# Storing a bias table's rows 128 times to read them on a diagonal, in place of products with a flipped identity

## The chip, the cores and the metric

The kernel runs on one core of a Trainium2 chip. The core has a matrix engine (TensorE, PE in the profile), a vector engine (VectorE, DVE), an activation engine (ScalarE, ACT), a general engine (GpSimd, POOL) and a sync engine (SyncE, SP), which here does little but issue transfers. Each engine works through its own list of instructions in order; semaphores hold an instruction until what it needs is there. Transfers between the memory of the chip (DRAM) and the on-chip memory (SBUF, 128 partitions) are carried by 16 DMA engines.

The metric is the device time of one execution, in microseconds, the median over several runs.

## The reference, cut to what matters

One layer of an encoder over 512 tokens of width 2048, float32. Two branches run side by side: a gated linear recurrence in eight heads, and an attention that lets each query see the 128 keys that an indexer picks for it. The change touches one term of the attention only, the bias by relative position:

```python
bias_table = rel_bias.astype(F32)                      # 32 buckets x 8 heads
...
logits = jnp.einsum('bthd,btkhd->bthk', q_blk, k_sel).astype(F32) * B_HEAD_DIM ** -0.5
bias = jnp.moveaxis(bias_table[t5_bucket(top_idx - t_pos[None, :, None])], -1, 2)
logits = jnp.where(valid[:, :, None, :], logits + bias, -jnp.inf)
```

For a head, the bias of query t and key s depends on s - t alone, and beyond a certain distance it is constant. So a row of 384 values per head holds all that is not constant, and a block of 128 queries by 256 keys needs that row shifted by one place from query to query: B[p, c] = row[127 - p + c].

## The kernel before, in words

All matrix products are made in pieces that keep float32 precision: each operand is split into a high and a low half, and three products (high x high, high x low, low x high) are summed in PSUM. The lines 74 to 76 are these three products, line 79 a single one. The halves of a weight piece are made by ACT (line 70, the high half) and DVE (line 71, the low half) from a raw tile (`wr`, two of them) that SP loads in line 127. The split halves have three places. A raw tile's next load is issued when DVE has made the low half of the piece that was in it; a piece is split while PE works on the piece two before it.

The program is one list of jobs, each a large product. Between the pieces of a job a function `pump` is called, which issues loads, flushes stores that were put off (`late`), and takes one step of each of several lanes: the recurrence's heads (`hgrn`), the top-k of the indexer (`top`), the attention (`att`), norms, and `t5`, the bias table. The lanes' instructions so fall between the products in the engines' lists, in the order in which Python emits them; nothing reorders them later.

The bias table is made while PE works on the jobs `ai_job(3)`, `ai_job(2)`, `af_aq(0)` and `af_aq(1)`, whose pieces are 48 products of 256 columns or 24 of 512 columns. At the same time the head pairs 3 and 2 of the recurrence run (tiles `hl`, `hz`, `hq`, `hqk`), and DVE runs the rounds of top-k (MAX and MATCH_REPLACE on tile `M`). The lane `t5` does this: it makes the eight rows by a product with one-hot buckets (lines 436 to 440, tile `tl`, 8 partitions x 384), splits them, stores both halves in DRAM, reads them back with the query's index as the partition (line 450; a pitch of one element between the partitions, so that partition p starts at element p), and multiplies by a flipped identity (line 457), since the wanted shift falls with p instead of rising. The result, a block of 128 x 256 for each of eight heads, goes to DRAM (`bh_d`, line 460). There are four rounds of two heads each, a pair of products in each.

Later the attention of each head loads its block (line 964), and POOL adds it to the mask (lines 968 and 971).

## Time and profile before

| | |
|---|---|
| median of 3 runs | 1338.1 us (1338.05 to 1338.66) |
| the profiled execution, its own time | 1337.35 us |
| its span in the profile | 1335.5 us |
| TensorE busy | 1324.8 us, 99% |
| VectorE busy | 1066.9 us, 80% |
| ScalarE busy | 669.2 us, 50% |
| GpSimd busy | 35.6 us, 3% |
| share of the chain that ended last on PE | 96% |
| bytes moved by the transfers | 205.82 MB |

The profile is of one execution. Its page gives the busy time of each engine, the transfers by queue, and the chain of work that ended last, followed back from the last instruction: an engine's share of that chain says how far it sets the time. The rows of a view in order of time give start and duration in us, engine, line, operation, the tiles written and read, and in brackets how long the engine stood idle before and what ended that. "SPq" rows are the issues of transfers, not the transfers themselves. Buffer numbers are left out of names, so that `t_d` is the tensor `t5_d`, `t` the lane's PSUM bank, and `hl`, `hz` banks of the recurrence.

### The profile page before, as it was taken

How to read it: one execution, taken by the hardware profiler on the slowest of the kernel's cores; microseconds unless marked ns; L12 is line 12 of the kernel's file. 1: busy time of each engine (PE TensorE's matmuls, PEld its weight loads, DVE VectorE, ACT ScalarE, POOL GpSimd, SP SyncE). 2: the span in 40 equal slices, each digit the busy share in tenths (PEclk: the TensorE clock that was granted, in tenths of full speed). 3: DMA queues.
4: the chain of work that ended last, by engine and by line, in shares of the span. 5: the costliest groups of instructions: out<-in, count | busy, mean ns of one | idle time of the engine just before them, and what ended most of it. 6: DMA issues, size and time to landing. Idle time of an engine off the chain costs nothing.

```text
span 1335.5 us, 26569 instructions
## 1 busy us (share of the span) xinstructions
PE 1324.8 (99%) x10876; PEld 1233.8 (92%) x10876; DVE 1066.9 (80%) x1705; ACT 669.2 (50%) x1064; POOL 35.6 (3%) x54
## 2 busy tenths in 40 slices
PE   9999999999999999999999999999999999999997
PEld 8988999999999999999999888888888888899996
DVE  7777888998888888886778988875656758899856
ACT  6455555554454444444666465656434423444435
POOL 2000000000000000000000000021001000000000
PEclk9999999999999999999999999999999999999999
DMA  6344545443454444434523624445655556643564
GB/s 241 92 113 115 158 142 159 144 142 111 143 158 143 142 143 142 130 111 163 184 86 102 182 76 155 132 144 182 239 192 191 186 175 219 204 160 126 164 209 163
DMA packets 141290, 205.82 MB, mean 154 GB/s; under 512 B 8672, under 2 KB 82032, under 8 KB 141040
## 3 DMA queue, kind: packets, MB, share of 16 engines
q1 hardware_dynamic: 140592, 203.78, 48.2%
q8 instruction: 85, 1.39, 0.4%
q10 hardware_dynamic: 576, 0.35, 0.1%
q14 instruction: 37, 0.30, 0.1%
HBM read 168.42 MB, written 35.68 MB: 153 GB/s over the span
## 4 chain that ended last, share of the span: by engine, by line
PE 96%; DVE 2%; DMA 1%; ACT 1%; issue 0%; SPq 0%; DVEq 0%; ACTq 0%
PE pp L76 15%; PE pp L74 15%; PE pp L75 15%; PE acc L74 14%; PE acc L76 14%; PE acc L75 14%; PE hl L79 1%; PE ho L79 1%; DMA xt<-in_x_t_dram 1%; PE sc L75 1%; PE sc L74 1%; PE sc L76 1%; DVE xl L338 0%; PE hp L79 0%; PE po L76 0%; PE po L75 0%
## 5 line engine op out<-in xcount | busy, mean ns | idle before, releaser
L149 ACT ACTIVATE bh<-wr 128x768 fp32r<-128x768 f32 x128 | 108.2, 846 | 208.5 <-issue 99.8
L151 ACT ACTIVATE wh<-sv 128x512 fp32r<-128x512 f32 x256 | 152.6, 624 | 86.1 <-DVE sv L144 65.5
L74 PE MATMUL pp<-sh,wh 128*128 128x256 f32 x618 | 170.6, 276 | 0.0
L75 PE MATMUL pp<-sl,wh 128*128 128x256 f32 x618 | 170.6, 276 | 0.0
L76 PE MATMUL pp<-sh,wl 128*128 128x256 f32 x618 | 170.6, 276 | 0.0
L71 DVE TENSOR_TENSOR wl<-wr,wh 128x1024 fp32r<-128x1024 f32 (+1 forms) x104 | 125.4, 1207 | 56.3 <-ACT wh L70 56.3
L153 DVE TENSOR_TENSOR wl<-sv,wh 128x1024 fp32r<-128x1024 f32 x128 | 156.4, 1222 | 6.3 <-ACT wh L151 0.3
L152 DVE TENSOR_TENSOR bl<-wr,bh 128x768 fp32r<-128x768 f32 x128 | 122.2, 954 | 43.4 <-ACT bh L149 43.2
L70 ACT ACTIVATE wh<-wr 128x1024 fp32r<-128x1024 f32 (+1 forms) x104 | 108.2, 1040 | 92.2 <-PE acc L75 44.1
L74 PE MATMUL acc<-xh,wh 128*128 128x512 f32 x304 | 120.3, 396 | 0.0
L76 PE MATMUL acc<-xh,wl 128*128 128x512 f32 x304 | 118.5, 390 | 0.0
L75 PE MATMUL acc<-xl,wh 128*128 128x512 f32 x304 | 118.5, 390 | 0.0
L75 PEld LDWEIGHTS pp<-sl,wh 128*128 128x128 f32 x618 | 116.0, 188 | 0.0
L76 PEld LDWEIGHTS pp<-sh,wl 128*128 128x128 f32 x618 | 116.0, 188 | 0.0
L74 PEld LDWEIGHTS pp<-sh,wh 128*128 128x128 f32 x618 | 116.0, 188 | 0.0
L74 PE MATMUL pp<-xh,bh 128*128 128x256 f32 x416 | 114.8, 276 | 0.0
L76 PE MATMUL pp<-xh,bl 128*128 128x256 f32 x416 | 114.8, 276 | 0.0
L75 PE MATMUL pp<-xl,bh 128*128 128x256 f32 x416 | 114.8, 276 | 0.0
L74 PE MATMUL acc<-yh,wh 128*128 128x512 f32 x256 | 100.3, 392 | 0.0
L75 PE MATMUL acc<-yl,wh 128*128 128x512 f32 x256 | 99.7, 390 | 0.0
L76 PE MATMUL acc<-yh,wl 128*128 128x512 f32 x256 | 99.7, 389 | 0.0
L144 DVE TENSOR_TENSOR sv<-wr 128x512 f32<-128x512 f32 x128 | 87.8, 686 | 9.0 <-DMA wr<-in_w_in_dram 6.5
(404 smaller groups left out, 3612.2 us busy)
## 6 DMA issues: line engine op xcount, KB each, us to landing
wr<-in_w_in_dram SPq DMA_DIRECT2D x136, 512.0 KB, 3.7
wr<-in_w_out_dram SPq DMA_DIRECT2D x32, 512.0 KB, 3.8
mg<-gate_d SPq DMA_DIRECT2D x48, 256.0 KB, 4.1
gate_d<-c SPq DMA_DIRECT2D x44, 256.0 KB, 4.9
wr<-in_w_in_dram SPq DMA_DIRECT2D x36, 256.0 KB, 3.0
wr<-in_w_pa_dram SPq DMA_DIRECT2D x16, 512.0 KB, 4.8
wr<-in_w_pb_dram SPq DMA_DIRECT2D x16, 512.0 KB, 3.9
wr<-in_w_qidx_dram SPq DMA_DIRECT2D x8, 512.0 KB, 3.7
```

The source lines that it names most:

```text
L70: A.activation(hi, src, AF.Copy)
L71: V.tensor_tensor(lo, src, hi.bitcast(F32), op=OP.subtract)
L74: PE.matmul(ps, lh, rh, start=first, stop=False, skip_group_check=True)
L75: PE.matmul(ps, lh, rl, start=False, stop=False, skip_group_check=True)
L76: PE.matmul(ps, ll, rh, start=False, stop=last, skip_group_check=True)
L79: PE.matmul(ps, l, r, start=first, stop=last, skip_group_check=True)
L144: V.tensor_tensor(sv[:, 0:2, :], b[:, 1:3, :], b[:, 0:1, :].to_broadcast([128, 2, 256]), op=OP.add)
L149: A.activation(bh, b[:, 1:4, :], AF.Copy)
L151: A.activation(vh[:, i:i + 2, :], sv[:, i:i + 2, :], AF.Copy)
L152: V.tensor_tensor(bl, b[:, 1:4, :], bh.bitcast(F32), op=OP.subtract)
L153: V.tensor_tensor(vl, sv, vh.bitcast(F32), op=OP.subtract)
```

## The change

The lane `t5` ends earlier. The rows `tl` are not split; one transfer stores each of them 128 times, into a DRAM tensor of 1024 rows of 384 elements. A head then reads its block from there with a pitch of 383 elements from partition to partition, starting at element 127 of its first copy: element p * 383 + 127 + c is element 127 - p + c of copy p. The flipped identity, its load and the eight products with it, the eight reads in the lane, four copies out of PSUM and four stores go.

```diff
-    t5_d = dram.tile([2, H, 384], F32, name="t5_d")
+    t5_d = dram.tile([H * 128, 384], F32, name="t5_d")
...
-    bh_d = dram.tile([H, 128, 256], F32, name="bh_d")
...
-        raw = R.i.tile([128, 512], F32, name="nt", bufs=2)
-        SP.dma_start(raw[:, 0:384], c_buckets)
-        SP.dma_start(raw[:, 384:], c_flip)
...
-        A.activation(flip, raw[:, 384:], AF.Copy)
...
         V.tensor_scalar(tl, ps[:H, :384], far, None, op0=OP.subtract)
         yield
-        split(*ts, tl)
-        for i in range(2):
-            late[1].append(lambda i=i: SP.dma_start(t5_d[i], ts[i].bitcast(F32)))
-        for _ in range(3):
-            yield
-        for h in range(0, H, 2):
-            bf = R.i.tile([128, 2, 2, 256], FR, name="bf")
-            for i in range(2):
-                SP.dma_start(bf[:, i].bitcast(F32), bass.AP(tensor=t5_d.tensor, offset=t5_d.offset + (i * H + h) * 384,
-                                                            ap=[[1, 128], [384, 2], [1, 256]]))
-            yield
-            yield
-            yield
-            ps = bank("t5")
-            for i in range(2):
-                mm(ps, flip, bf[:, i].rearrange("p h c -> p (h c)"), i == 0, i == 1)
-            e = R.i.tile([128, 2, 256], F32, name="nt", bufs=2)
-            V.tensor_copy(e, ps.rearrange("p (h c) -> p h c", h=2))
-            late[1].append(lambda h=h, e=e: SP.dma_start(bh_d[h:h + 2].rearrange("h p c -> p h c"), e))
-            yield
+        late[1].append(lambda: SP.dma_start(t5_d.rearrange("(h p) c -> h p c", h=H), tl.unsqueeze(1).to_broadcast([H, 128, 384])))
+        yield
...
         bh = R.a.tile([128, 256], F32, name="bh")
-        SP.dma_start(bh, bh_d[h])
+        SP.dma_start(bh, bass.AP(tensor=t5_d.tensor, offset=t5_d.offset + h * 128 * 384 + 127, ap=[[383, 128], [1, 256]]))
```

SP's list at the place of the table, before (`wr` are weight loads, `hg` a load of gates for the recurrence):

```order
L426 DMA rb<-in_rel_bias_dram 32x8
L428 DMA nt<-in_buckets_dram 128x384
L429 DMA nt<-in_flip_dram 128x128
L127 DMA wr<-in_w_in_dram 128x4x256 x3
L444 DMA t_d<-tlh 8x384
L444 DMA t_d<-tll 8x384
L450 DMA bf<-t_d 128x2x256 x2
L127 DMA wr<-in_w_in_dram 128x4x256 x2
L450 DMA bf<-t_d 128x2x256 x2
L127 DMA wr<-in_w_in_dram 128x4x256
L460 DMA bh_d<-nt 128x2x256
L127 DMA wr<-in_w_in_dram 128x4x256
```

and now, where the lines above the change have moved up by one and those below by 23:

```order
L423 DMA rb<-in_rel_bias_dram 32x8
L425 DMA raw<-in_buckets_dram 128x384
L126 DMA wr<-in_w_in_dram 128x4x256 x3
L437 DMA t_d<-tl 1024x1x384
L126 DMA wr<-in_w_in_dram 128x4x256 x5
L718 DMA hg<-gate_d 128x2x512
```

The wide store stands where the two small ones stood, behind the third of these weight loads, and the next five weight loads follow it with nothing between.

ACT's list a little later, now, is as it was but for the line numbers (`hz` to `hqk` and the two after it are steps of a recurrence head, `hv` is the result of the last piece of `ai_job(2)`):

```order
L70 ACTIVATE hzh<-hqk 128x512 x2
L70 ACTIVATE wh<-wr 128x1024
L871 ACT_TABLE_LOAD
L876 ACTIVATE hqk<-hz,cols 128x512 x2
L877 ACTIVATE hqk<-hqk 128x1024
L70 ACTIVATE wh<-wr 128x1024
```

Here nothing moved: the high half of a weight piece stands ahead of the head's steps, before as now.

## The prediction

> **What bounds the kernel now.** I read the head of the page first, then the chain of waits, then the stretch in which the bias table is made.

> ```profile
> span 1335.5 us, 26569 instructions
> ...
> PE 1324.8 (99%) x10876; PEld 1233.8 (92%) x10876; DVE 1066.9 (80%) x1705; ACT 669.2 (50%) x1064; POOL 35.6 (3%) x54
> ...
> q1 hardware_dynamic: 140592, 203.78, 48.2%
> ...
> PE 96%; DVE 2%; DMA 1%; ACT 1%; issue 0%; SPq 0%; DVEq 0%; ACTq 0%
> ```

> TensorE sets the end: it is busy for 99% of the span and 96% of the chain that ended last is its own work. An edit gains only what it takes out of PE's stream, and loses whatever makes PE stand still. The stretches around the bias table (columns: time, then the busy us of PE, of the weight loads, of DVE, ACT and POOL) show the second thing to watch:

> ```profile
> 690.00:863.00 173.00, 173.00 (x2236) 151.77 (x2235) 149.63 (x289) 99.76 (x151) 2.85 (x5) 1.00 0.42 126
> 722.00:753.00 31.00, 31.00 (x270) 28.97 (x270) 29.96 (x73) 15.53 (x22) 0.00 (x0) 1.00 0.48 135
> ```

> PE never stands still there, but between 722 and 753 us DVE is busy for 29.96 of 31.00 us. Whatever holds DVE up in that stretch can't be caught up before PE next needs it.

> **What the change removes.** On PE eight products with the flipped identity, in four pairs. Instructions by form for their bank, then PE in order of time around the second pair:

> ```profile
> L79 PE MATMUL t<-bf,flip x8: 392/392/503, 728.7 to 768.4; 128*128 128x512 f32 x8
> L459 DVE COPY nt<-t x4: 679/681/714, 730.9 to 770.0; 128x512 f32<-128x512 f32 x4
> ```

> ```profile
> 741.08 0.62 PE L79 MATMUL t<-bf,flip 128*128 128x512 f32 x2
> 741.54 0.28 PE L74 MATMUL acc<-wh,xh 128*128 128x256 f32 x1
> ```

> The 392 ns of one product is its way through the array and overlaps the next; what the pair costs is the distance to the following start, 741.54 - 741.08 = 0.46 us. Four pairs: **1.85 us off PE**. (The other three stand behind short products, after which the next start is late with or without them; I take 0.46 for each.) On DVE four copies of 0.68 us go, on ACT and DVE the flip's copy and one split, on SP fifteen transfers: eight reads and four stores of 256 KB, two stores of 12 KB, the flip's load:

> ```profile
> bf<-t_d SPq DMA_DIRECT2D x8, 256.0 KB, 4.3
> ...
> bh_d<-nt SPq DMA_DIRECT2D x4, 256.0 KB, 4.3
> ...
> t_d<-tlh SPq DMA_DIRECT2D x1, 12.0 KB
> ```

> Beside these products, which go themselves, PE waits for none of that in this stretch, so it is worth nothing by itself; the copy at 744.69 us will matter below, since it shortens DVE's queue by 0.68 us.

> **What it adds.** One transfer: 8 rows of 1536 bytes, each written 128 times, 1024 pieces and 1.57 MB, issued from eight partitions where nearly all others move 128. SP's queue in order of time (start, duration, line; x2 joins two issues, here at 722.10 and 728.20), and a weight load's time to landing:

> ```profile
> 713.34 0.37 SPq L127 DMA_DIRECT2D wr<-in_w_in_dram  x1
> 713.75 0.44 SPq L444 DMA_DIRECT2D t_d<-tlh  x1
> 714.25 0.29 SPq L444 DMA_DIRECT2D t_d<-tll  x1
> ```

> ```profile
> 717.49 0.90 SPq L450 DMA_DIRECT2D bf<-t_d  x2
> 722.10 6.48 SPq L127 DMA_DIRECT2D wr<-in_w_in_dram  x2
> 735.80 0.37 SPq L127 DMA_DIRECT2D wr<-in_w_in_dram  x1
> ```

> ```profile
> wr<-in_w_in_dram SPq DMA_DIRECT2D x136, 512.0 KB, 3.7
> ```

> The new store takes the place of the two small ones, at 713.75 us. The load of 713.34 is ahead of it and lands near 713.34 + 3.7 = 717.0, so the store's bytes flow from about 716.5 us. The next weight load (722.10, call it A) and the one after it (728.20, B) stand behind it in the same queue.

> How long does it take? The page's queue row gives 0.482 x 16 x 1335.5 us / 140592 = 73 ns for a mean packet of 1449 bytes, that is 19.8 GB/s for one engine's stream, and 79 us for the store if it came out as one stream, 40 as two, 20 as four, 9.9 as eight. **Bounds:** not under 9.9 us, since eight source rows make at most eight streams of that kind; not much over 79 us, since in the ordinary 128-row transfers each of 16 streams serves eight rows, so that one stream is what this trace has seen come out of eight rows. Nothing wide of the trace comes from so few rows; the two 12 KB stores are too small to tell. Between ends eight-fold apart I take the middle, between two and four streams: **28 us**, from 716.5 to 744.6 us.

> [...]

> **Who waits for A.** ACT turns A into its high half, DVE into its low half, PE multiplies with both. ACT, PE and DVE in order of time:

> ```profile
> 723.29 1.05 ACT L70 ACTIVATE wh<-wr 128x1024 fp32r<-128x1024 f32 x1
> ...
> 732.17 1.06 ACT L70 ACTIVATE wh<-wr 128x1024 fp32r<-128x1024 f32 x1 [1.06 <-PE acc L76]
> 733.25 1.28 ACT L894 ACT_TABLE_LOAD   x1
> ```

> ```profile
> 744.36 0.39 PE L74 MATMUL acc<-xh,wh 128*128 128x512 f32 x1
> ```

> ```profile
> 752.61 0.73 PE L79 MATMUL hl<-hq,hqk 128*32 128x32 f32 x62
> ```

> ```profile
> 734.56 1.22 DVE L71 TENSOR_TENSOR wl<-wr,wh 128x1024 fp32r<-128x1024 f32 x1
> ...
> 744.69 0.68 DVE L459 COPY nt<-t 128x512 f32<-128x512 f32 x1
> ...
> 748.75 1.22 DVE L748 TENSOR_TENSOR hqk<-hq,hf 128x1024 f32<-128x1024 f32 x1
> ```

> Two raw weight tiles exist, so the ACT split at 723.29 is of the other tile and the one at 732.17 is of A. It waits there for the end of a piece of PE's (three split tiles exist), hence its result is for the piece after the next two, which PE starts at 744.36. A's 512 packets are 32 on each engine, 32 x 73 ns = 2.3 us. With the store's end at 744.6 A is in at 746.9 instead of at 722.10 + 3.7 = 725.8. ACT is in order: it stands from 732.2 to 746.9, with the table load and the four ACT steps of the head in progress queued behind. DVE stands at its own half of A from 734.6 on, with the top-k rounds, the scaling of the heads and L748 behind it. Then:

> - ACT's half is done at 746.9 + 1.06 = 748.0, DVE's at 748.0 + 1.22 = 749.2, where before it was 735.8: DVE is 13.4 us late.
> - PE, by then 0.9 us early by two pairs, wants A at 743.4 and waits about 5 us; it runs one piece and half of the next (about 8.5 us of products) and comes to the products of L79 that stood at 752.61. They need DVE's L748, which ended at 749.97; now 749.97 + 13.4 - 0.68 (the copy that is gone) = 762.7.
> - PE resumes 762.7 - 752.6 = 10.1 us later than before. Two pairs of the four still come: 0.9 us back. **Net loss 9.2 us.**

> After that PE sets the pace again: DVE waits for L79's products before its next scaling, and its lateness is PE's. What PE lost is not regained, since it has no idle time to give up.

> In general, for a store of L us the net is L - 18.9, as long as that is above -1.85: A lands within what ACT and DVE have to spare up to L = 17, and a loss over 0.2% of the time needs L over 21.6.

> **The bias reads.** The heads read 128 rows of 1 KB at a pitch of 1532 bytes instead of 1024: same count, same bytes.

> ```profile
> L964 SPq DMA_DIRECT2D bh<-bh_d x8: 418/450/528, 864.9 to 1042.6; - x8
> ...
> DMA to landing us min/median/max: 3.2/4.3/6.8
> ```

> ```profile
> POOL MB L968 <- DMA bh<-bh_d: 146.0, 6, 33.1
> ```

> Only POOL waits for them, which works for 3% of the span and whose sums are asked for two steps of the pump later. Should every read take double the 4.3 us, POOL still starts within the 33 us that it idles now. Worth nothing; without that cover it would be 4.3 us for each of eight heads. The first read, at 864.9 us, is 120 us behind the store's end.

> **Sum.** The profiled execution took 1337.35 us, 0.75 below the median of 1338.1. 1337.35 + 9.2 = 1346.6; against the median, **1347.3 us**. Its own range, with L from 22 to 33 us, is 1341 to 1352.

> **Rivals.**

> *The store hides* (not slower). Each source row is served as a stream of its own, L = 9.9, the store ends at 726.4, A is in by 729 and ACT finds it at 732.2. What is left is the 1.85 us off PE: 1336.2 us. For it: the other stores reach such speeds, and nothing shows a limit at the source rows. Against: no transfer in the trace has drawn on so few rows. It decides up to L = 17. [...]

> *A store in between*, L from 17 to 21.6: the loss eats the gain, 1336.2 to 1340.8 us.

> *One stream*, L = 79: the store ends near 796, A is 50 us later than in the forecast, and each us is PE's: about 1398 us. Little speaks for it, since eight rows going out through one stream would need the transfer to be dealt out by rows as the wide ones are.

> *Faster than the products alone explain*: 5 us of DVE, ACT and SP work goes from the densest stretch of DVE, and with a hidden store PE might find a step ready sooner. But PE stood still nowhere between 690 and 863 us, so there is nothing to find; it would need 0.8 us more, to 1335.4.

> **How the numbers follow.** About 0.2%, 2.7 us, is what a measurement of this kernel tells from no change. On the scale of streams, the doublings from 9.9 to 79 us put about six tenths above 21.6 and four below; I give the forecast 0.59, the single stream 0.04, the store in between 0.05, the hidden store 0.28 and the faster variant 0.04. Slower is 0.59 + 0.04 = 0.63, same 0.05 + 0.28 = 0.33, faster 0.04. The range takes in the hidden store at the one end and the forecast's own range at the other: 1335.7 to 1352; what is left out is the single stream, the faster variant and the forecast's edge.

> **What would show it.** In the changed kernel's profile: the store's time to landing, 28 us or so for right, near 12 for the hidden store. ACT's split near 732 us with some 15 us of idle time before it, put down to the weight load. PE with two gaps, about 5 us near 743 and a similar one at the products of L79 some 10 us later. If ACT finds A on time and PE has no gap, the length of the store was wrong. If the store is long and PE still has no gap, then the order of transfers in the queue was: A would have passed the store.

## The result, and the profile after

| | kernel before | changed kernel |
|---|---|---|
| median | 1338.07 us (1337.17 to 1338.66, 4 runs) | 1350.37 us (1349.81 to 1350.51, 4 runs) |
| profiled execution, its own time | 1337.35 us | 1350.3 us |
| span | 1335.5 us | 1348.5 us |

The ratio is 1.0092, with a 95% interval of 1.0074 to 1.0109: the change costs 12.3 us. The forecast was a loss of 9.2 us, to 1347.3 us, with a range of 1335.7 to 1352.

The head of the page of the changed kernel, and the engines' shares of the chain that ended last:

```profile
span 1348.5 us, 26522 instructions
...
PE 1327.6 (98%) x10868; PEld 1235.0 (92%) x10868; DVE 1063.5 (79%) x1700; ACT 668.1 (50%) x1062; POOL 38.1 (3%) x54
...
PE 92%; DVE 3%; DMA 3%; ACT 1%; issue 0%; SPq 0%; DVEq 0%; ACTq 0%
```

PE has eight products fewer and yet is busy longer, its share of the chain fell from 96 to 92%, and DMA has 3% of it instead of 1. The stretches by engine, in the same columns as before (time, busy us of PE, weight loads, DVE, ACT, POOL, then the granted clock, the share of DMA and GB/s):

```profile
690.00:863.00 173.00, 161.90 (x2166) 141.39 (x2165) 137.97 (x274) 86.45 (x133) 2.85 (x5) 0.97 0.40 106
722.00:753.00 31.00, 23.76 (x190) 22.36 (x189) 13.40 (x39) 7.75 (x13) 0.00 (x0) 0.90 0.48 74
```

PE stands for 11.1 of the 173 us in which it never stood before; 7.2 of them lie between 722 and 753 us, where DVE, busy for 29.96 us before, is now busy for 13.40.

**The store.** SP's queue in order of time, and the transfers between 713 and 770 us (in this view the stretch is cut in 40 slices of 1.425 us; the DMA row has the busy tenths of 16 engines, the row below what they moved):

```profile
706.32 6.66 SPq L126 DMA_DIRECT2D wr<-in_w_in_dram  x2
713.04 0.84 SPq L437 DMA_DIRECT2D t_d<-tl  x1
722.07 43.03 SPq L126 DMA_DIRECT2D wr<-in_w_in_dram  x5
```

```profile
DMA  4954444446944447744444445300660008400899
GB/s 80 313 74 46 50 49 49 49 49 86 197 56 52 49 49 118 163 47 51 46 50 49 49 102 176 126 11 0 142 237 0 0 0 226 142 0 0 197 231 282
```

From the third slice, about 716 us, to the twenty-fourth, about 747 us, a floor of 46 to 52 GB/s does not move: this is the store, and 1.57 MB at 50 GB/s are 31 us. About 4 tenths of the engines, that is seven or eight, are busy with it. On this floor stand two bursts, in the tenth and eleventh slice (725.8 to 728.7 us) and in the sixteenth and seventeenth. Each adds some 260 KB to the floor, about half of a load's 512 KB: I read them as those parts of A and of the load behind it that lie on the other eight engines. Their parts on the store's engines come only with the burst at its end, from the twenty-fourth slice to the twenty-sixth (746 to 750 us).

**The wait for A.** ACT, then DVE, in order of time:

```profile
729.92 1.15 ACT L70 ACTIVATE hzh<-hqk 128x512 fp32r<-128x512 f32 x2
749.94 1.06 ACT L70 ACTIVATE wh<-wr 128x1024 fp32r<-128x1024 f32 x1 [18.86 <-DMA wr<-in_w_in_dram]
751.01 1.28 ACT L871 ACT_TABLE_LOAD   x1
```

```profile
751.02 1.22 DVE L71 TENSOR_TENSOR wl<-wr,wh 128x1024 fp32r<-128x1024 f32 x1 [17.01 <-ACT wh L70]
...
764.63 1.22 DVE L725 TENSOR_TENSOR hqk<-hq,hf 128x1024 f32<-128x1024 f32 x1
```

This is the split that stood at 732.17 before; the 18.86 us in the brackets are ACT's, with the table load behind it, and 17.01 are DVE's. L725 is the line that was L748: it ends at 765.85, before at 749.97.

**What PE does.** In order of time:

```profile
743.80 0.28 PE L76 MATMUL acc<-wh,xl 128*128 128x256 f32 x1
751.05 0.80 PE L74 MATMUL acc<-xh,wh 128*128 128x512 f32 x1 [6.97 <-ACT wh L70]
...
764.22 0.76 PE L79 MATMUL hl<-hq,hqk 128*32 128x32 f32 x64 [1.68 <-ACT hqk L724]
765.90 0.74 PE L79 MATMUL hl<-hqk 128*32 128x16 f32 x64 [0.91 <-DVE hqk L725]
...
773.03 0.74 PE L79 MATMUL hl<-hq 128*32 128x16 f32 x64 [0.74 <-ACT hq L781]
774.29 0.74 PE L79 MATMUL hl<-hqk 128*32 128x16 f32 x64 [0.52 <-DVE hqk L758]
```

PE waits five times, 10.8 us together: 6.97 for A's high half, then 1.68 and 0.91 at the products of L79 that ran at 752.61 before, and 0.74 and 0.52 at the next such step.

### The profile page after: what moved, and what is told of

The parts are those of the page before. It is cut to its first block, busy times and chain, and to the rows that moved or that the text cites. A ratio compares the mean times of both kernels' runs of the same rounds, so it can differ in the third digit from the quotient of the medians.

```text
span 1348.5 us, 26522 instructions
## 1 busy us (share of the span) xinstructions
PE 1327.6 (98%) x10868; PEld 1235.0 (92%) x10868; DVE 1063.5 (79%) x1700; ACT 668.1 (50%) x1062; POOL 38.1 (3%) x54
## 4 chain that ended last, share of the span: by engine, by line
PE 92%; DVE 3%; DMA 3%; ACT 1%; issue 0%; SPq 0%; DVEq 0%; ACTq 0%
PE pp L76 15%; PE pp L74 15%; PE pp L75 15%; PE acc L74 13%; PE acc L75 13%; PE acc L76 13%; DMA wr<-in_w_in_dram 2%; PE hl L79 1%; DMA xt<-in_x_t_dram 1%; PE ho L79 1%; PE sc L75 1%; PE sc L74 1%; PE sc L76 1%; DVE wl L71 0%; DVE xl L337 0%
## 5 line engine op out<-in xcount | busy, mean ns | idle before, releaser
L71 DVE TENSOR_TENSOR wl<-wr,wh 128x1024 fp32r<-128x1024 f32 (+1 forms) x104 | 125.4, 1207 | 71.9 <-ACT wh L70 71.9
L74 PE MATMUL pp<-sh,wh 128*128 128x256 f32 x618 | 170.6, 276 | 0.0
L76 PE MATMUL pp<-sh,wl 128*128 128x256 f32 x618 | 170.6, 276 | 0.0
L70 ACT ACTIVATE wh<-wr 128x1024 fp32r<-128x1024 f32 (+1 forms) x104 | 108.1, 1040 | 105.8 <-PE acc L75 41.6
L74 PE MATMUL acc<-xh,wh 128*128 128x512 f32 x304 | 121.8, 401 | 7.0 <-ACT wh L70 7.0
L76 PE MATMUL acc<-xh,wl 128*128 128x512 f32 x304 | 119.7, 394 | 0.0
L76 PEld LDWEIGHTS pp<-sh,wl 128*128 128x128 f32 x618 | 116.0, 188 | 0.0
L74 PEld LDWEIGHTS pp<-sh,wh 128*128 128x128 f32 x618 | 116.0, 188 | 0.0
L74 PE MATMUL pp<-xh,bh 128*128 128x256 f32 x416 | 114.8, 276 | 0.0
L76 PE MATMUL pp<-xh,bl 128*128 128x256 f32 x416 | 114.8, 276 | 0.0
L74 PE MATMUL acc<-yh,wh 128*128 128x512 f32 x256 | 100.3, 392 | 0.0
L76 PE MATMUL acc<-yh,wl 128*128 128x512 f32 x256 | 99.7, 389 | 0.0
## 6 DMA issues: line engine op xcount, KB each, us to landing
wr<-in_w_in_dram SPq DMA_DIRECT2D x136, 512.0 KB, 3.6
wr<-in_w_out_dram SPq DMA_DIRECT2D x32, 512.0 KB, 3.8
mg<-gate_d SPq DMA_DIRECT2D x48, 256.0 KB, 4.4
gate_d<-c SPq DMA_DIRECT2D x44, 256.0 KB, 4.9
wr<-in_w_in_dram SPq DMA_DIRECT2D x36, 256.0 KB, 3.0
wr<-in_w_pa_dram SPq DMA_DIRECT2D x16, 512.0 KB, 4.8
wr<-in_w_pb_dram SPq DMA_DIRECT2D x16, 512.0 KB, 4.1
wr<-in_w_qidx_dram SPq DMA_DIRECT2D x8, 512.0 KB, 3.3
```

The source lines that it names most:

```text
L70: A.activation(hi, src, AF.Copy)
L71: V.tensor_tensor(lo, src, hi.bitcast(F32), op=OP.subtract)
L74: PE.matmul(ps, lh, rh, start=first, stop=False, skip_group_check=True)
L76: PE.matmul(ps, ll, rh, start=False, stop=last, skip_group_check=True)
```

## The experiments

Each kernel is compared with the kernel before on the same chip, whose median there was 1337.45 us (27 runs, for the first four kernels) or 1337.65 us (14 runs, for the others). The diffs are against the changed kernel.

### The same bytes from 128 partitions

```diff
-        tl = R.i.tile([H, 384], F32, name="tl")
+        tl = R.i.tile([128, 384], F32, name="tl")
...
-        split(*rbs, rb)
+        split(*(r.rearrange("p (h j) -> p h j", h=H) for r in rbs), rb[:, :, None].to_broadcast([128, H, 16]))
...
-            mm(ps[:H, :384], r, oh, i == 0, i == 1)
+            mm(ps[:128, :384], r, oh, i == 0, i == 1)
...
-        late[1].append(lambda: SP.dma_start(t5_d.rearrange("(h p) c -> h p c", h=H), tl.unsqueeze(1).to_broadcast([H, 128, 384])))
+        late[1].append(lambda: SP.dma_start(t5_d.rearrange("(q r) c -> q r c", r=8), tl.unsqueeze(1).to_broadcast([128, 8, 384])))
```

> The changed kernel with the eight rows made on 128 partitions, 16 of each (the one-hot product takes sixteen copies of each bucket column), so that every partition stores its row 8 times: the same 1024 pieces of 1536 bytes, the same reads at a pitch of 383. Theory (a store drawn from eight neighbouring partitions is slow, 232 ns per piece on eight engines, and the weight loads behind it in SP's queue hold ACT, DVE and PE up): pieces back at 65 ns, 64 of them on each of 16 engines, 4 to 5 us in all; ACT finds its weights at 732 us; no gap on PE; only the removed products are left, 1338.1 - 1.85 = 1336.2 us. Rival (the amount written, or the reads at a pitch of 383, is what costs): both are as they were, so 1350 us.

Measured: 1336.03 us (1335.34 to 1336.70, 11 runs), ratio 0.9989 [0.9981, 0.9998]. The transfers between 713 and 770 us, and ACT's split of A:

```profile
GB/s 7 171 370 401 407 126 1 30 295 43 0 2 218 160 0 0 11 257 99 0 0 46 290 43 0 37 254 262 318 404 380 188 14 83 297 0 0 0 0 129
...
t_d<-tl SPq DMA_DIRECT2D x1, 1536.0 KB, 8.4
```

```profile
732.64 1.06 ACT L70 ACTIVATE wh<-wr 128x1024 fp32r<-128x1024 f32 x1 [0.70 <-PE acc L76]
```

The same 1024 pieces, with the load ahead of them, move at up to 407 GB/s and are through before 722 us (1.57 MB at 400 GB/s are about 4 us). ACT again waits for PE and not for the load, and PE waits nowhere in the stretch. The loss is gone with the length of the store alone. This version takes 1.4 us less than the kernel before, and the interval of the ratio ends just below 1.

### The eight rows four partitions apart

```diff
-        tl = R.i.tile([H, 384], F32, name="tl")
+        tl = R.i.tile([32, 384], F32, name="tl")
...
-        late[1].append(lambda: SP.dma_start(t5_d.rearrange("(h p) c -> h p c", h=H), tl.unsqueeze(1).to_broadcast([H, 128, 384])))
+        late[1].append(lambda: SP.dma_start(t5_d.rearrange("(h p) c -> h p c", h=H), tl[0:32:4].unsqueeze(1).to_broadcast([H, 128, 384])))
```

> The changed kernel with the eight rows on partitions 0, 4, 8 to 28 in place of 0 to 7: still eight source rows, each stored 128 times, so still eight streams. Theory that neighbouring partitions share a way out (groups of four): each stream has its own now, 128 pieces of 65 to 67 ns, 8.6 us, hidden: 1336.2 us. Rival, that eight streams are slow whatever their rows, or that one row's many readings are: about 31 us again and 1350 us.

Measured: 1336.05 us (1335.03 to 1336.88, 10 runs), ratio 0.9989 [0.998, 0.9998].

```profile
DMA  0595555593007500084002820289999604900004
GB/s 0 93 303 203 199 200 204 204 317 129 0 0 172 206 2 0 0 221 147 0 0 21 284 75 0 22 225 266 313 407 384 225 15 55 320 4 0 0 11 78
```

Still one row for each of eight partitions, and still half of the engines (5 tenths), but 200 GB/s instead of 50. So the eight source rows, or eight engines, do not make the store slow: that the rows lie next to each other does.

### The store on ACT's queue

```diff
-        late[1].append(lambda: SP.dma_start(t5_d.rearrange("(h p) c -> h p c", h=H), tl.unsqueeze(1).to_broadcast([H, 128, 384])))
+        late[1].append(lambda: A.dma_start(t5_d.rearrange("(h p) c -> h p c", h=H), tl.unsqueeze(1).to_broadcast([H, 128, 384])))
```

> The changed kernel with the same store from eight neighbouring partitions issued by ACT, in whose queue nothing else stands, in place of SP. The theory's second half (what costs is that the weight loads stand behind the store in one queue): the store still takes about 30 us, but the engines take pieces of both queues in turn, so that a load's 32 pieces on an engine need 32 x (232 + 46) ns = 9 us, and the load of 722 us is in by about 732 us: 1336 to 1339 us. Rival (the engines, or the source rows' way out, are taken up and every load is late whatever its queue): 1347 to 1351 us.

Measured: 1345.85 us (1344.65 to 1346.41, 4 runs), ratio 1.0059 [1.0044, 1.0075]. The time lies between the two expectations, 1.2 us below the second, and its interval, 1343.3 to 1347.5 us, reaches into that one. ACT in order of time, SP's queue, the transfers between 713 and 770 us, and PE's waits between 700 and 800 us (us in total, times, longest):

```profile
710.47 1.28 ACTq L437 DMA_DIRECT2D t_d<-tl  x1
...
738.04 1.06 ACT L70 ACTIVATE wh<-wr 128x1024 fp32r<-128x1024 f32 x1 [13.41 <-DMA wr<-in_w_in_dram]
745.85 1.06 ACT L70 ACTIVATE wh<-wr 128x1024 fp32r<-128x1024 f32 x1 [3.77 <-DMA wr<-in_w_in_dram]
```

```profile
707.59 0.37 SPq L126 DMA_DIRECT2D wr<-in_w_in_dram  x1
...
713.89 0.37 SPq L126 DMA_DIRECT2D wr<-in_w_in_dram  x1
```

```profile
GB/s 51 84 195 49 49 49 47 49 156 125 52 85 75 82 81 80 77 76 79 79 190 161 159 61 0 72 295 1 0 0 162 216 2 0 125 245 314 407 403 321
```

```profile
PE hz L79 <- ACT hzh L70: 5.8, 1, 5.8
PE hz L79 <- DVE hzl L71: 1.4, 1, 1.4
```

The store is issued 2.6 us earlier (710.47 instead of 713.04), ahead of the load that SP issues at 713.89. In the changed kernel that load (712.62 there, the second of the two in the row of 706.32) went before the store; here it is late itself, and its split stands at 738.04. The row of GB/s shows how it came in. Until about 728 us there is the store's floor of 49 GB/s with bursts on it: in the second and third slice, by the same reading as above, the load's part on the free engines goes, the rest does not move. Only from the twelfth slice on (728.7 us) does the rate rise to 75 to 85 GB/s and stay there: I read this as the rest of the load, moving between the store's pieces. Some 31 GB/s above the floor are about 30 pieces of 1 KB per us beside the store's 32 of 1536 bytes, so about one for one. So from another queue this load did get past the store, but only 14 us after it was issued. Why not at once can't be read from these runs. At 49 GB/s the store moves 32 pieces per us, four on each of eight engines, so 14 us are some 56 pieces on each; that the engines had taken up so many of them before the load came is an explanation, not shown.

The loss here is 8.4 us over the kernel before on this chip, so 3.9 of the 12.3 us came back. How much of that the other queue gave stays open, since the store was also issued 2.6 us earlier.

### Each row stored once

```diff
-    t5_d = dram.tile([H * 128, 384], F32, name="t5_d")
+    t5_d = dram.tile([H, 384], F32, name="t5_d")
...
-        late[1].append(lambda: SP.dma_start(t5_d.rearrange("(h p) c -> h p c", h=H), tl.unsqueeze(1).to_broadcast([H, 128, 384])))
+        late[1].append(lambda: SP.dma_start(t5_d, tl))
...
-        SP.dma_start(bh, bass.AP(tensor=t5_d.tensor, offset=t5_d.offset + h * 128 * 384 + 127, ap=[[383, 128], [1, 256]]))
+        SP.dma_start(bh, bass.AP(tensor=t5_d.tensor, offset=t5_d.offset + h * 384, ap=[[1, 128], [1, 256]]))
```

> The changed kernel with each row stored once (12 KB in all) and each head's block read with a pitch of one element upwards from it; left out is the direction of the shift, so that a query's bias is that of another query. It has neither the products with the flipped identity nor the wide store: the gain alone. By four times 0.46 us on PE: 1338.1 - 1.85 = 1336.2 us. Rival (DVE, ACT and SP are also relieved in their densest stretch): 1335.4 us or less. Rival (the removed products cost PE nothing, since they filled time that it waits anyway): 1338 us.

Measured: 1335.89 us (1335.13 to 1336.64, 10 runs), ratio 0.9989 [0.998, 0.9998]; the span is 1334.0 us. Without the wide store the removal alone is left: 1.56 us by the medians, 1.5 by the spans, for the 1.85 of the working, which lies within the interval (0.3 to 2.7 us). The rival without any gain lies outside it; the rival of a larger gain, 2.7 us or more, only at its edge. Reads at a pitch of one element and reads at 383 (the kernel from 128 partitions) end within 0.15 us of each other.

### Half and three quarters of the copies

```diff
-    t5_d = dram.tile([H * 128, 384], F32, name="t5_d")
+    t5_d = dram.tile([H * 64, 384], F32, name="t5_d")
...
-        late[1].append(lambda: SP.dma_start(t5_d.rearrange("(h p) c -> h p c", h=H), tl.unsqueeze(1).to_broadcast([H, 128, 384])))
+        late[1].append(lambda: SP.dma_start(t5_d.rearrange("(h p) c -> h p c", h=H), tl.unsqueeze(1).to_broadcast([H, 64, 384])))
...
-        SP.dma_start(bh, bass.AP(tensor=t5_d.tensor, offset=t5_d.offset + h * 128 * 384 + 127, ap=[[383, 128], [1, 256]]))
+        SP.dma_start(bh, bass.AP(tensor=t5_d.tensor, offset=t5_d.offset + min(h * 64, H * 64 - 128) * 384 + 127, ap=[[383, 128], [1, 256]]))
```

The second kernel has 96 in the place of 64.

> The changed kernel with each row stored 64 times in place of 128, from the same eight partitions (left out: half of the copies; the heads read as before, from rows that partly belong to the next head, so some biases are another head's). The changed kernel's pieces take 0.242 us each on an engine, 128 of them 31 us; 64 take 15.5 us, from 715.6 to 731 us, and the load behind them is in near 734, 0.6 us of DVE's lateness, less than it has to spare. Theory (a store is free up to some 17 us and each us above costs one): 1336.2 us, no gap on PE. Rival (the loss is in proportion to the store, 14.2 us for 31 us): 1338.1 - 1.85 + 7.1 = 1343.3 us.

> The same with 96 copies (a quarter left out): 23.2 us, from 715.6 to 738.8 us; the load behind is in near 742, about 8 us after ACT asks for it. Theory (free up to some 17 us, then one for one): 7.8 us less store than the changed kernel, so 1350.4 - 7.8 = 1342.6 us. Rival (in proportion): 1336.2 + 14.2 x 0.75 = 1346.9 us.

Measured: with 64 copies 1335.92 us (1335.43 to 1337.18, 10 runs), ratio 0.9988 [0.9979, 0.9998]; with 96 copies 1342.37 us (1341.06 to 1342.59, 5 runs), ratio 1.0033 [1.002, 1.0047]. ACT's split of A with 64 copies:

```profile
733.71 1.06 ACT L70 ACTIVATE wh<-wr 128x1024 fp32r<-128x1024 f32 x1 [2.27 <-DMA wr<-in_w_in_dram]
```

The same with 96 copies, and PE's waits there:

```profile
741.06 1.06 ACT L70 ACTIVATE wh<-wr 128x1024 fp32r<-128x1024 f32 x1 [9.70 <-DMA wr<-in_w_in_dram]
```

```profile
PE hl L79 <- ACT hqk L724: 2.6, 1, 2.6
PE hl L79 <- DVE hqk L725: 0.7, 1, 0.7
```

With 64 copies A is 1.5 us later at ACT than before (733.71 against 732.17), and PE does not wait for it. With 96 it is 8.9 us later, and PE stands at the products of L79. The loss is not in proportion to the bytes: the first half of the store is free, and what comes after it counts. At 50 GB/s 96 copies take 23.6 us, and the working's net of L - 18.9 makes 4.7 us of it; 1342.37 - 1337.65 = 4.7.

That the two agree so closely is partly luck, for PE's waits with 96 copies are only 3.3 us. The rest lies in the granted clock, the third number from the end of the first row below. PE in order of time follows, with 96 copies and then before:

```profile
752.00:764.00 12.00, 8.68 (x149) 6.81 (x148) 11.76 (x22) 5.28 (x7) 0.00 (x0) 0.72 0.68 215
```

```profile
757.03 1.05 PE L79 MATMUL hl<-hqk 128*32 128x16 f32 x64 [0.72 <-DVE hqk L725]
...
765.79 0.70 PE L79 MATMUL hl<-hq 128*32 128x16 f32 x62
```

```profile
753.20 0.70 PE L79 MATMUL hl<-hqk 128*32 128x16 f32 x62
...
759.97 0.71 PE L79 MATMUL hl<-hq 128*32 128x16 f32 x62
```

The second run of L79's products is 3.8 us late. From it to the next step PE needs 8.76 us, where it needed 6.77 with a pair of flip products in between (0.46): 2.4 us go to products at the lower clock. 3.8 + 2.4 - 0.9 for the two later pairs make 5.3 us, and the spans differ by 5.3 (1340.8 and 1335.5). So less is lost by lateness than the working says, and the clock, which it does not have, adds the rest.

### Sixteen rows, and eight rows sixteen partitions apart

Two kernels on what makes neighbouring rows slow; the tile `tl` and the product that fills it are made 16 and 128 partitions wide, as above. In the first the table has each row twice, on partitions 0 to 15, and each of them is stored 64 times; in the second the eight rows lie on the partitions 0, 16, 32 to 112.

```diff
-        late[1].append(lambda: SP.dma_start(t5_d.rearrange("(h p) c -> h p c", h=H), tl.unsqueeze(1).to_broadcast([H, 128, 384])))
+        late[1].append(lambda: SP.dma_start(t5_d.rearrange("(q r) c -> q r c", r=64), tl.unsqueeze(1).to_broadcast([16, 64, 384])))
```

```diff
-        late[1].append(lambda: SP.dma_start(t5_d.rearrange("(h p) c -> h p c", h=H), tl.unsqueeze(1).to_broadcast([H, 128, 384])))
+        late[1].append(lambda: SP.dma_start(t5_d.rearrange("(h p) c -> h p c", h=H), tl[0:128:16].unsqueeze(1).to_broadcast([H, 128, 384])))
```

> The changed kernel with the eight rows made on partitions 0 to 15, two of each, so that each of 16 partitions stores its row 64 times: four groups of four neighbours in place of two. Theory (four neighbours share one way out, on which a piece takes about 60 ns): four ways, still 232 ns a piece for each of four streams that share one, 64 of them: 15 us in place of 31, about 100 GB/s in place of 51; hidden, 1336.2 us. Rival (twice the engines are busy, but the rate of the source rows is what it is for them all): 31 us, 51 GB/s and 1350 us.

> The changed kernel with the eight rows on partitions 0, 16, 32 to 112. If only four direct neighbours share a way out, each row has its own: 200 GB/s for 8.6 us as with rows four apart. If partitions 32 apart share one too, two rows stand on each of four ways: about 116 ns a piece, 105 GB/s for 15 us. The time is 1336.2 us by both, since up to some 17 us are hidden.

Measured: 1336.62 us each, one run. The transfers between 713 and 770 us with sixteen rows on partitions 0 to 15:

```profile
DMA  0798888888888990066000840098999901910005
GB/s 0 143 341 107 96 98 97 95 98 97 98 97 118 366 356 24 0 153 215 0 0 4 240 135 0 3 180 228 318 408 405 282 33 23 310 47 0 0 11 109
```

and with eight rows sixteen partitions apart:

```profile
DMA  0775444595448851038000670069999920840005
GB/s 4 183 263 162 94 98 96 116 241 121 94 97 172 272 178 42 0 57 305 6 0 0 138 241 0 0 110 211 294 401 411 356 73 0 218 155 6 0 0 125
```

## Why the prediction was right, and where it was off

**The store, 28 us: right in kind, a tenth too short.** That was the choice between 9.9 and 79 us; 31 us were measured. The bounds held for this store (eight rows four partitions apart, at 200 GB/s, took 7.9 us, less than the lower one), but what stood behind the choice, how many streams eight rows make, is not what decides: seven or eight engines carried the store, for which the working had 9.9 us, and it took 31. That the middle of an eight-fold span of guesses came within 3 us of it was luck.

**A in at 746.9: 3.0 us too early, the term that was mis-sized.** ACT began at 749.94. Of these 3 us the store's longer time is most. Part of it is also that not A alone stood behind the store: by the reading of the GB/s row above, the load after it too had half of its pieces on the store's engines, and both came in the burst of 746 to 750 us.

**DVE's lateness: right.** DVE's half of A ended 3.0 us later than predicted (752.24 for 749.2), and its L748 3.15 us later (765.85 for 762.7). The queue behind the wait is the one named, less the copy that went.

**PE's two waits: the places right, the sizes not.** The first was 6.97 us instead of about 5, since A was later. The second was not as long again but 2.6 us (1.68 and 0.91), although DVE was later than predicted. What filled the difference is a thing that the prediction didn't have. Here is the granted clock after, in the columns of the windows above:

```profile
744.00:752.00 8.00, 1.03 (x3) 0.50 (x2) 0.97 (x1) 2.04 (x2) 0.00 (x0) 0.68 0.35 85
752.00:764.00 12.00, 10.50 (x35) 7.94 (x34) 11.69 (x27) 7.41 (x11) 0.00 (x0) 0.79 0.30 89
764.00:775.00 11.00, 8.60 (x281) 7.04 (x281) 10.79 (x19) 3.21 (x4) 0.00 (x0) 1.00 0.76 239
```

and PE in order of time within the second of these stretches:

```profile
753.33 0.63 PE L75 MATMUL acc<-xl,wh 128*128 128x512 f32 x1
753.75 0.63 PE L76 MATMUL acc<-xh,wl 128*128 128x512 f32 x1
...
757.38 0.40 PE L76 MATMUL acc<-xh,wl 128*128 128x512 f32 x1
757.62 0.39 PE L74 MATMUL acc<-xh,wh 128*128 128x512 f32 x1
...
762.15 0.39 PE L76 MATMUL acc<-xh,wl 128*128 128x512 f32 x1
```

After its wait PE ran until about 757 us with products 0.42 us apart, where they are 0.23 apart before and later. The 36 products from the one wait to the other, which the prediction put at about 8.5 us, had their first start at 751.05 and their last at 762.15, 11.1 us, where before they took from 744.36 to

```profile
752.30 0.39 PE L76 MATMUL acc<-xh,wl 128*128 128x512 f32 x1
```

that is 7.9. The 3.2 us of slow products cost nothing here: DVE, busy for 11.69 of the 12.00 us by the row above, was not ready, and PE would have waited instead. With 96 copies PE waited for nothing at the end of such products, and there they did cost 2.4 us.

**The net of 9.2 us: 13.0 by the spans, 12.3 by the medians.** (The profiled execution before was 0.7 below its median, the one after was not.) By the steps: the second run of L79's products, for which DVE is needed, started at 765.90, before at

```profile
753.20 0.70 PE L79 MATMUL hl<-hqk 128*32 128x16 f32 x62
```

which is 12.7 later where the working has 10.1: 2.6 us more. DVE's L748 is 3.15 us later than the working has it; 0.6 of that goes off again, since the working held it against the first run of L79's products (752.61), and the second run, 0.6 us behind, is the one that waits for it. The two later pairs give 0.9 back. Then PE waits twice more for the recurrence, 0.74 and 0.52 us, which the sentence "After that PE sets the pace again" left out: DVE was still behind, busy for 10.79 of the 11.00 us from 764 on. 12.7 - 0.9 + 1.3 = 13.1. From there on nothing is regained, as predicted.

With the measured 31 us the formula L - 18.9 makes 12.1 us, 1350.2 for the measured 1350.37, and it fits the stores up to 17 us as well. So the mechanism was right, and the term that was mis-sized is the store. The small terms that the formula lacks are the two later waits here and the lower clock with 96 copies; that its 4.7 us for these copies is the measured one too is partly luck.

**The bias reads at nothing: right.**

```profile
bh<-t_d SPq DMA_DIRECT2D x8, 128.0 KB, 4.0
```

```profile
POOL MB L945 <- DMA bh<-t_d: 173.9, 7, 32.7
```

They land in 4.0 us (4.3 before), and only POOL waits for them, now 173.9 us in seven waits, with PE still set by its own stream.

**The rivals.** The hidden store fell with A's 18.86 us at ACT. It is what the stores from 128 partitions, from partitions four apart, and from half of the copies show: at about 4 to 15.7 us they leave 1336.0 us, and the rival said 1336.2. The single stream, 79 us, is out by the floor of 50 GB/s. *The store in between* is what 96 copies come near to, with a loss of 4.7 us for 23.6 us of store. *Faster than the products alone* is not seen: the row stored once gains 1.56 us, less than the products' 1.85, though its interval reaches to 2.7. The order of transfers was as named: the GB/s row shows no more than half of a load passing the store, some 260 KB of 512.

## What to carry to other kernels

Ask of a wide transfer from few partitions not only how many bytes, pieces and engines it has, but which partitions its rows lie on: the same bytes took about 4, 8, 16 and 31 us here (by rates of some 400, 200, 97 and 50 GB/s) with nothing but the rows' places changed. If such a transfer is off the critical path, its own time does not matter, but what stands behind it in the same queue does: find the first load behind it that the bound engine needs, and how much later that load may land; up to there the transfer is free, beyond it nearly every us counted here (the last quarter of the copies, 7.9 us of store, cost 7.6). Another queue was no full way out (3.9 of the 12.3 us came back, with the store issued 2.6 us earlier); to lay the rows apart, or to repeat them in the product that makes them, returned it all, at no cost that the times show.

## What the runs showed of the hardware that was not expected

- The store, slow on seven or eight engines, held back about half of each of the two loads behind it, while the other half, some 260 KB, went through. In the GB/s row of the changed kernel A's first half is seen at 725.8 to 728.7 us, some 20 us before the rest; it was of no use, since ACT began with A only at 749.94. The issues of these two loads were held too: they took 3.86 and 5.79 us, where the issue at 713.34 before took 0.37.
- The granted clock of TensorE fell in the wait of 6.97 us: 0.68 from 744 to 752 us, 0.79 from 752 to 764, with products 0.42 us apart until about 757 us. It is only by the later wait for DVE that this did not add to the loss. With 96 copies, where PE waited 2.6 and 0.7 us, it was 0.72 from 752 to 764 us, and there it cost 2.4 us. After the waits of 1.68 and 0.91 us in the changed kernel the clock stayed at 1.00 from 764 to 775 us.
- With the store on ACT's queue the rest of SP's load came in beside it, some 31 GB/s above the store's floor of 49, but for the load issued at 713.89 us not before 728.
